# A gated recurrence's levels sent to TensorE in pairs, with a second pair of operand tiles

## The chip, the cores and the metric

The kernel runs on one core of one Trainium2 chip, in one launch. The metric is the device time of one execution in microseconds; the figure of a kernel is the median of several runs. A profiled execution gives the trace, whose own time and span (from the first to the last instruction) are given below. Engines are named as in the profile: PE is TensorE, PEld its weight loads, DVE is VectorE, ACT is ScalarE, POOL is GpSimd, SP is SyncE, which issues the transfers.

## The reference

One layer over 256 tokens of width 1024: an embedding layer norm, one input projection `w_in` into the columns of four causal mixers (Mamba-2 SSD, HGRN2, RetNet retention, MoBA attention), each with four heads of 64 and a gate, then one output projection, a residual and a layer norm. The part that the change touches, cut down:

```python
# HGRN2: S_t = diag(f_t) S_{t-1} + (1 - f_t) i_t^T, o_t = S_t^T q_t
att = einsum('bhtd,bhsd,bhtsd->bhts', q, k, exp(b_t - b_s))   # s <= t, b = cumsum(log f)
o   = einsum('bhts,bhsv->bhtv', att, v) + (carry of earlier chunks)

# SSD: causal depthwise convolution over 4 taps, then silu
xbc = silu(conv(xbc_raw, conv_w) + conv_b)

# MoBA, one block of 256 here: softmax over the causal scores with ALiBi
p = softmax(q k^T * d**-0.5 - slope * (t - s))
```

## The kernel before

**Slots.** The input projection is cut into 30 slots, two for each of 15 units of weights (`h_f`, `h_q`, `h_i`, `m_q`, `m_k`, `xs`, `bc`, `zv` twice, `r_q`, `r_k`, `r_v`, `m_g`, `gg` twice); eight more slots lie in the output projection. A slot is `begin(slot)` and then `project(slot)`. `begin` issues the load of the weights six slots ahead (`load_w`, SP), rounds the weights four slots ahead into a high part (`split_hi`, one cast on ACT, line 225), runs the list `steps[slot]`, and takes the low part on DVE (`split_lo`, line 234). `project` is 24 matmuls on PE (line 420; 12 a slot for the wide units `zv` and `gg`, line 381). The order of each engine's instructions is this program order, written out by hand in the table `steps`. Nothing overtakes on an engine: an instruction that waits holds all that is behind it there.

**The recurrence.** HGRN2's attention matrix is built by doubling. `A` (query side) and `B` (the tile `kk`, key side) hold operands decayed to block borders; `Fm[m]` holds the products of gates over blocks of m. `level(m)`, `level32`, `level64` and `level128` are the matmuls of B with A that give the entries between neighbouring blocks of m tokens; `widen(m)` multiplies half of A and half of B in place by the gates of the neighbouring block (three DVE operations, lines 524, 525 and 528), after which they stand for 2m. So the chain is widen, level, widen, level, and each widen has to wait until the level before it has read its operands. `level_in(m)` (DVE, line 552) writes the entries of a level into `att`; `level32_in` (ACT, lines 569 and 572) copies `att` and level 32 into `yh`; `level64_in` and `level128_in` (ACT, lines 587 and 600) copy the last two levels into `yh` and `l128`. `hgrn_av` in slot 20 reads `yh` and `l128`.

**The other steps near it.** `conv(n, name)` is one step on ACT (line 654, scale and bias from the PSUM bank of the projection), followed by three taps on DVE (line 656); four of these, then `conv_silu` on ACT (line 660). `moba_max(T)` is DVE (line 849), `moba_exp(T)` ACT (line 860), which waits for it, `moba_scale(T)` DVE (line 877). `ssd_step_a` is one small DVE operation (line 681) and two small exponentials on ACT (lines 682 and 683), the second of which waits for it. `moba_v` (line 833) copies the second half of the projection `zv` over the tile `kk`.

**PSUM.** All results of PE lie in one pool `pp` of 8 tiles, one bank each. A new tile takes the bank whose last reader comes first in program order, and its first matmul waits for that reader. `bank(...)` and `pp.tile(...)` are the allocations. Each level takes two banks (one for each parity of the head).

Of the kernel before, what the change touches and what calls it, by code (L numbers as in the profile page):

```python
# [17 lines left out]
P = 128  # L18
SEQ = 256
# [103 lines left out]
def hybrid_layer(  # L123
# [13 lines left out]
    nc = tc.nc  # L137
# [318 lines left out]
    f = sb([P, 2, SEQ], "f")  # L456
    kk = sb([P, 2, SEQ], "kk")
    A = sb([P, 2 * SEQ], "A")
    qk = sb([P, 2, SEQ], "qk", tag="s2a")
    B = flat(kk)  # L460
    Fm = {1: flat(f)}
    att = sb([P, 8, 64], "att", tag="att")
    hb = {}
# [17 lines left out]
    def hgrn_query():  # L481
        for n in range(2):
            nc.vector.tensor_mul(qk[:, n, :], hq[n], kk[:, n, :])
        for n in range(2):
            nc.vector.tensor_mul(A[:, n * SEQ:(n + 1) * SEQ], hq[n], f[:, n, :])
        nc.vector.tensor_mul(flat(e1)[:, 0::2], A[:, 1::2], B[:, 0::2])

# [28 lines left out]
    def hix(T, h):  # L516
        return (h % 2) * 4 + T * 2 + h // 2

    def widen(m):
        nb = 2 * SEQ // (2 * m)  # L520
        Fv = Fm[m].rearrange("p (b two) -> p b two", two=2)
        Av = A.rearrange("p (b two m) -> p b two m", two=2, m=m)
        Bv = B.rearrange("p (b two m) -> p b two m", two=2, m=m)
        nc.vector.tensor_mul(Av[:, :, 1, :], Av[:, :, 1, :], Fv[:, :, 0:1].to_broadcast([P, nb, m]))
        nc.vector.tensor_mul(Bv[:, :, 0, :], Bv[:, :, 0, :], Fv[:, :, 1:2].to_broadcast([P, nb, m]))
        if m < 64:
            Fn = sb([P, nb], f"F{2 * m}")
            nc.vector.tensor_mul(Fn, Fv[:, :, 0], Fv[:, :, 1])
            Fm[2 * m] = Fn

    def ab(t, h, lo_, n_):
        r = 64 * (h % 2)
        o = (h // 2) * SEQ + lo_
        return t[r:r + 64, o:o + n_]

    def level(m):
        bs = [bank(f"lv{m}{par}") for par in range(2)]
        for T in range(NT):
            for n in range(2):
                for c in range(2):  # L540
                    for par in range(2):
                        o = T * P + c * 64
                        q = (T * 2 + n) * 64
                        h = 2 * n + par
                        nc.tensor.matmul(bs[par][c * 64:c * 64 + 64, q:q + 64],  # L545
                                         ab(B, h, o, 64), ab(A, h, o, 64), start=True, stop=True)
        hb[m] = bs

    def level_in(m):
        i = (1, 2, 4, 8, 16).index(m)  # L550
        for par in range(2):
            nc.vector.copy_predicated(att[:, par * 4:par * 4 + 4, :],
                                      lev[:, i, :].unsqueeze(1).to_broadcast([P, 4, 64]),
                                      heads(hb[m][par][:, 0:256]))

    def level32():
        hb[32] = [heads(bank(f"lv32{par}")) for par in range(2)]
        for T in range(NT):
            for n in range(2):
                for c in range(2):  # L560
                    for par in range(2):
                        o = T * P + c * 64
                        h = 2 * n + par
                        nc.tensor.matmul(hb[32][par][c * 64:c * 64 + 32, T * 2 + n, 32:64],
                                         ab(B, h, o, 32), ab(A, h, o + 32, 32), start=True, stop=True)

    def level32_in():
        for c in range(2):
# [15 lines left out]

    def level64_in():
        for par in range(2):
            nc.scalar.copy(yh[0:64, par * 4:par * 4 + 4, 64:128], heads(hb[64][par][par * 64:par * 64 + 64, 0:256]))

    l128 = sb([P, 4, P], "l128")

    def level128():
        hb[128] = [bank(f"lv128{par}") for par in range(2)]
        for n in range(2):
            for par in range(2):
                nc.tensor.matmul(hb[128][par][:, n * P:(n + 1) * P], ab(B, 2 * n + par, 0, P),
                                 ab(A, 2 * n + par, P, P), start=True, stop=True)

    def level128_in():
        for par in range(2):
            nc.scalar.copy(l128[:, par * 2:par * 2 + 2, :],  # L600
                           hb[128][par][:, 0:256].rearrange("p (a t) -> p a t", t=P))

    hv = sb([P, NT, DB], "hv", tag="hv")
    ho = sb([P, 8, HD], "ho")
# [410 lines left out]
    def out_norm(T):  # L1015
# [12 lines left out]
        for n, c in enumerate(range(0, DM, st)):  # L1028
# [8 lines left out]
    steps = {  # L1037
        0: [lambda: hgrn_gate(0), lambda: hgrn_gate(1)],
        1: [hgrn_key],
        4: [hgrn_query, lambda: widen(1)],  # L1040
        6: [moba_load],
        7: [lambda: hgrn_diag(qk, 0), lambda: hgrn_diag(e1, 8), lambda: level(2), h_values,
            hgrn_diag_in],
        8: [lambda: level_in(2), lambda: widen(2), moba_q],
        9: [lambda: level(4), lambda: widen(4)],
        10: [lambda: level_in(4), lambda: level(8), moba_k],
        11: [lambda: level_in(8), lambda: widen(8)],
        12: [lambda: level(16), lambda: moba_scores(0), lambda: conv(0, "xs")],
        13: [lambda: moba_max(0, (0, 1, 2, 3)), lambda: moba_exp(0, (0, 1, 2, 3)), ssd_step_a,
             lambda: level_in(16), lambda: widen(16), lambda: conv(1, "xs")],  # L1050
        14: [level32, lambda: moba_scores(1), lambda: conv(2, "bc"), level32_in],
        15: [lambda: moba_max(1, (0, 1)), lambda: moba_max(1, (2, 3)), lambda: moba_exp(1, (0, 1, 2, 3)),
             lambda: widen(32), lambda: conv(3, "bc"), lambda: moba_scale(0)],
        16: [level64, lambda: widen(64), lambda: conv_silu("xs", 0), lambda: conv_silu("bc", 2),
             level64_in, lambda: moba_scale(1)],
        17: [lambda: load_rows(0), ssd_step_b],
        18: [level128, ssd_scores, lambda: moba_tr(0), lambda: moba_tr(1), moba_v, level128_in,
             lambda: z_in(0), lambda: z_in(1), ssd_scores_in, lambda: moba_tr_in(0), lambda: moba_tr_in(1)],
        20: [ssd_xt, ssd_seg, ssd_exp, lambda: moba_tr(2), lambda: hgrn_av(0), lambda: hgrn_av(1),
             lambda: moba_tr_in(2), ret_load],  # L1060
# [92 lines left out]
```

## Time and profile before

| | us |
|---|---|
| median of 3 runs (149.34 to 149.35) | 149.35 |
| profiled execution, its own time | 149.55 |
| its span | 147.8 |
| PE busy | 136.7 |
| DVE busy | 116.3 |
| ACT busy | 75.1 |

Busy time counts instructions, not waits. The profiled execution takes 1.75 us more than its span, and 0.2 us more than the median. The mean granted clock of TensorE is 0.982 of full speed.

### The profile page before, as it was taken

To read this page: it belongs to the slowest core of one execution; us is meant where nothing else is said; L and a number is where in the kernel's file an instruction comes from. 1 tells how busy PE (TensorE), PEld (TensorE's weight loads), DVE (VectorE), ACT (ScalarE), POOL (GpSimd) and SP (SyncE) were. 2 spreads that over 40 slices of the span, in tenths; PEclk is the share of its full clock that TensorE was granted. 3 is DMA by queue.
4 is the path that set the end of the run, shared out by engine and by line. 5 is a ranking of instruction groups with operands and counts; after the bars stand their busy time and mean duration, and the time that the engine had idled before them with its cause. 6 is when DMAs were issued, how large, how long until landed. Compare 5 with 4: busy or idle time off the path is not lost.

```text
span 147.8 us, 3075 instructions
## 1 busy us (share of the span) xinstructions
PE 136.7 (92%) x1224; PEld 122.4 (83%) x1224; DVE 116.3 (79%) x244; ACT 75.1 (51%) x122; POOL 16.0 (11%) x21
## 2 busy tenths in 40 slices
PE   5759999999999999999999999999999999999900
PEld 3159999999999998878899999999988888888900
DVE  1689978999597297969997599976989993959381
ACT  3079968662452759599808971035855655000000
POOL 4230000000000000000052009005002200002010
PEclk9977999999999999999999999999999999999997
DMA  4999299998758422494635740079874540000304
GB/s 146 287 381 361 63 302 356 299 344 316 217 153 248 143 48 94 142 244 190 162 119 146 265 163 4 0 231 357 278 233 156 162 155 0 0 0 0 142 0 142
DMA packets 9533, 26.05 MB, mean 176 GB/s; under 512 B 1072, under 2 KB 1968, under 8 KB 9264
## 3 DMA queue, kind: packets, MB, share of 16 engines
q1 hardware_dynamic: 9088, 25.35, 52.6%
q10 hardware_dynamic: 432, 0.52, 1.0%
q8 instruction: 9, 0.15, 0.4%
q14 instruction: 4, 0.03, 0.1%
HBM read 24.82 MB, written 1.05 MB: 175 GB/s over the span
## 4 chain that ended last, share of the span: by engine, by line
PE 82%; DVE 8%; DMA 3%; ACT 1%; SPq 1%; issue 1%; POOL 1%; DVEq 0%
PE po L996 15%; PE pj_gg L381 8%; PE pj_h_f L346 4%; PE pj_xs L420 4%; PE pj_m_k L420 4%; PE pj_m_g L420 4%; PE pj_r_k L420 4%; PE pj_m_q L420 4%; PE pj_h_i L420 4%; PE pj_zv L381 4%; PE pj_h_q L420 4%; PE pj_r_v L420 4%; PE pj_r_q L420 4%; DMA xt<-in_x_dram 3%; PE pj_bc L420 2%; PE lv L545 2%
## 5 line engine op out<-in xcount | busy, mean ns | idle before, releaser
L996 PE MATMUL po<-whi_wo,yhi 128*128 128x512 f32 (+1 forms) x40 | 14.0, 350 | 0.0
L996 PE MATMUL po<-wlo_wo,yhi 128*128 128x512 f32 (+1 forms) x40 | 14.0, 349 | 0.0
L996 PE MATMUL po<-whi_wo,ylo 128*128 128x512 f32 (+1 forms) x40 | 13.9, 348 | 0.0
L234 DVE TENSOR_TENSOR wlo_wo<-wr_wo,whi_wo 128x1024 fp32r<-128x1024 f32 x8 | 9.7, 1217 | 0.0
L225 ACT CAST whi_wo<-wr_wo 128x1024 fp32r<-128x1024 f32 x8 | 8.2, 1049 | 2.2 <-PE pj_gg L381 1.7
L996 PEld LDWEIGHTS po<-whi_wo,yhi 128*128 128x128 f32 x40 | 7.5, 188 | 1.1
L996 PEld LDWEIGHTS po<-wlo_wo,yhi 128*128 128x128 f32 x40 | 7.5, 188 | 1.0
L996 PEld LDWEIGHTS po<-whi_wo,ylo 128*128 128x128 f32 x40 | 7.5, 188 | 1.0
L710 POOL TENSOR_SCALAR_AFFINE_SELECT ra<-ahi 128x1024 fp32r<-128x1024 f32 x1 | 1.1, 1101 | 64.9 <-DVE ahi L706 64.9
L225 ACT CAST whi_zv<-wr_zv 128x1024 fp32r<-128x1024 f32 x4 | 4.2, 1048 | 6.8 <-PE pj_xs L420 3.4
L656 DVE SCALAR_TENSOR_TENSOR cacc_xs<-pj_xs,ch,cacc_xs 128x255 f32<-128x255 f32 (+2 forms) x6 | 2.9, 482 | 4.7 <-ACT cacc_xs L654 4.6
L381 PE MATMUL pj_zv<-whi_zv,hhi 128*128 128x512 f32 x16 | 6.5, 406 | 0.0
L179 PE MATMUL warm<-warm 128*128 128x512 f32 x6 | 5.1, 1011 | 1.5 <-DVE warm L176 1.5
L381 PE MATMUL pj_gg<-whi_gg,hhi 128*128 128x512 f32 x16 | 6.4, 398 | 0.0
L381 PE MATMUL pj_zv<-whi_zv,hlo 128*128 128x512 f32 x16 | 6.3, 394 | 0.0
L381 PE MATMUL pj_gg<-whi_gg,hlo 128*128 128x512 f32 x16 | 6.3, 394 | 0.0
L381 PE MATMUL pj_gg<-wlo_gg,hhi 128*128 128x512 f32 x16 | 6.3, 392 | 0.0
L381 PE MATMUL pj_zv<-wlo_zv,hhi 128*128 128x512 f32 x16 | 6.3, 392 | 0.0
L303 PE MATMUL tr<-ck,xn 128*128 128x128 f32 x16 | 3.7, 360 | 2.3 <-DVE xn L279 2.3
L303 PEld LDWEIGHTS tr<-ck,xn 128*128 128x128 f32 x16 | 2.6, 187 | 3.7 <-DVE xn L279 3.7
L225 ACT CAST whi_gg<-wr_gg 128x1024 fp32r<-128x1024 f32 x4 | 4.2, 1045 | 2.4 <-DMA wr_gg<-in_w_dram 1.6
L266 DVE BATCH_NORM_STATS2 lst<-xt 128x6 f32<-128x512 f32 x4 | 2.8, 694 | 3.2 <-DMA xt<-in_x_dram 3.2
(284 smaller groups left out, 490.4 us busy)
## 6 DMA issues: line engine op xcount, KB each, us to landing
wr_wo<-in_wo_dram SPq DMA_DIRECT2D x8, 512.0 KB, 3.9
wr_zv<-in_w_dram SPq DMA_DIRECT2D x4, 512.0 KB, 4.6
rb<-in_rows_dram SPq DMA_DIRECT2D x2, 1024.0 KB, 6.6
wr_gg<-in_w_dram SPq DMA_DIRECT2D x4, 512.0 KB, 4.9
wr_h_i<-in_w_dram SPq DMA_DIRECT2D x2, 520.0 KB, 5.2
xt<-in_x_dram SPq DMA_DIRECT2D x4, 256.0 KB, 3.5
wr_h_f<-in_w_dram SPq DMA_DIRECT2D x4, 256.0 KB, 4.7
wr_h_q<-in_w_dram SPq DMA_DIRECT2D x2, 512.0 KB, 5.5
```

The costliest lines, as they stand in the source:

```text
L179: nc.tensor.matmul(wb, warm[:, :P], warm, start=True, stop=True)
L225: copy(whi[i, j][:, r, :], t[:, r, :])
L234: nc.vector.tensor_sub(wlo[i, j][:, r, :], t[:, r, :], whi[i, j][:, r, :].bitcast(F32))
L266: nc.vector.bn_stats(lst[T][:, hf, :], xt[T][:, hf * 512:hf * 512 + 512])
L303: nc.tensor.transpose(trb[k][:, T * P:(T + 1) * P], xn[T][:, k * P:(k + 1) * P], ident)
L346: nc.tensor.matmul(ps[n], l[:, n * P:(n + 1) * P], r[:, k, :], start=(k == 0 and q == 0), stop=(k == KT - 1 and q == 2))
L381: nc.tensor.matmul(ps_of[name, T], l[:, k, ts], r, start=(k == 0 and q == 0), stop=(k == KT - 1 and q == 2))
L420: nc.tensor.matmul(ps, l, r, start=(n == 0), stop=(n == len(seq) - 1))
L545: nc.tensor.matmul(bs[par][c * 64:c * 64 + 64, q:q + 64], ab(B, h, o, 64), ab(A, h, o, 64), start=True, stop=True)
L656: nc.vector.scalar_tensor_tensor(a_[:, d:], ps[:, :SEQ - d], tap(3 - d), a_[:, d:], op0=ALU.mult, op1=ALU.add)
L710: nc.gpsimd.affine_select(out=t, in_=src.bitcast(F32).unsqueeze(2).to_broadcast([P, 8, P]), pattern=[[0, 8], [1, P]], compare_op=ALU.is_ge ...
L996: nc.tensor.matmul(po[T, c0], l[:, k, ts], r, start=(i == 0 and j == 0 and q == 0), stop=(last and q == 2), skip_group_check=(T == 1 and i ...
```

## The change

Three things in the source. First, the levels go to PE in pairs, 4 with 8, 16 with 32 and 64 with 128, each pair into one pair of banks (columns 0 to 255 and 256 to 511). Second, a second set of operands `AB[1]` (in the memory of the tile `ldec`, which is free until slot 20) takes every second widened pair: `widen(m, s, d)` reads set s and writes set d; where they differ, ACT copies the two halves that stay as they are. Third, the table of steps is rewritten: among other moves, `conv(1)` and `conv(3)` now stand before `moba_exp(0)` and `moba_exp(1)`, `ssd_step_a` after `conv(1)`, `level32_in` moves from slot 14 to 17, `level64` from 16 to 18.

```diff
-    def widen(m):
+    def widen(m, s, d):
         nb = 2 * SEQ // (2 * m)
+        if d == len(AB):
+            t = sb([P, 2, 2 * SEQ], "AB2", tag="ldec")
+            AB.append((t[:, 0, :], t[:, 1, :]))
...
+        if s != d:
+            nc.scalar.copy(Ad[:, :, 0, :], As[:, :, 0, :])
+            nc.scalar.copy(Bd[:, :, 1, :], Bs[:, :, 1, :])
+        nc.vector.tensor_mul(Ad[:, :, 1, :], As[:, :, 1, :], Fv[:, :, 0:1].to_broadcast([P, nb, m]))
+        nc.vector.tensor_mul(Bd[:, :, 0, :], Bs[:, :, 0, :], Fv[:, :, 1:2].to_broadcast([P, nb, m]))
...
+    def lv(m, after=None):
+        if after is None:
+            hb["b", m] = [bank(f"lv{m}{par}") for par in range(2)]
+        o = 0 if after is None else 256
+        hb[m] = [b[:, o:o + 256] for b in hb["b", m if after is None else after]]
+        return hb[m]
...
-        8: [lambda: level_in(2), lambda: widen(2), moba_q],
-        9: [lambda: level(4), lambda: widen(4)],
-        10: [lambda: level_in(4), lambda: level(8), moba_k],
-        11: [lambda: level_in(8), lambda: widen(8)],
-        12: [lambda: level(16), lambda: moba_scores(0), lambda: conv(0, "xs")],
-        13: [lambda: moba_max(0, (0, 1, 2, 3)), lambda: moba_exp(0, (0, 1, 2, 3)), ssd_step_a,
-             lambda: level_in(16), lambda: widen(16), lambda: conv(1, "xs")],
-        14: [level32, lambda: moba_scores(1), lambda: conv(2, "bc"), level32_in],
-        15: [lambda: moba_max(1, (0, 1)), lambda: moba_max(1, (2, 3)), lambda: moba_exp(1, (0, 1, 2, 3)),
-             lambda: widen(32), lambda: conv(3, "bc"), lambda: moba_scale(0)],
-        16: [level64, lambda: widen(64), lambda: conv_silu("xs", 0), lambda: conv_silu("bc", 2),
-             level64_in, lambda: moba_scale(1)],
-        17: [lambda: load_rows(0), ssd_step_b],
-        18: [level128, ssd_scores, lambda: moba_tr(0), lambda: moba_tr(1), moba_v, level128_in,
+        8: [lambda: widen(2, 0, 0), lambda: widen(4, 0, 1), lambda: level_in(2), moba_q],
+        10: [moba_k],
+        11: [lambda: level(4, 0), lambda: level(8, 1, 4), lambda: moba_scores(0),
+             lambda: level_in(4), lambda: level_in(8), lambda: widen(8, 1, 1)],
+        12: [lambda: conv(0, "xs"), lambda: widen(16, 1, 0), lambda: moba_max(0, (0, 1, 2, 3))],
+        13: [lambda: conv(1, "xs"), lambda: moba_exp(0, (0, 1, 2, 3)), ssd_step_a],
+        14: [lambda: level(16, 1), lambda: level32(0, 16), lambda: moba_scores(1),
+             lambda: conv(2, "bc"), lambda: widen(32, 0, 0), lambda: level_in(16)],
+        15: [lambda: widen(64, 0, 1), lambda: conv(3, "bc"), lambda: moba_max(1, (0, 1)),
+             lambda: moba_max(1, (2, 3)), lambda: moba_exp(1, (0, 1, 2, 3))],
+        16: [lambda: conv_silu("xs", 0), lambda: conv_silu("bc", 2), lambda: moba_scale(0),
+             lambda: moba_scale(1)],
+        17: [lambda: load_rows(0), level32_in, ssd_step_b],
+        18: [lambda: level64(0), lambda: level128(1), ssd_scores, lambda: moba_tr(0), lambda: moba_tr(1),
+             moba_v, level64_in, level128_in,
              lambda: z_in(0), lambda: z_in(1), ssd_scores_in, lambda: moba_tr_in(0), lambda: moba_tr_in(1)],
```

## Rows read from the trace of the kernel before

**Rows 1.** The page: part 1 (busy, share, instructions) and the chain by engine.

```profile
PE 136.7 (92%) x1224; PEld 122.4 (83%) x1224; DVE 116.3 (79%) x244; ACT 75.1 (51%) x122; POOL 16.0 (11%) x21
...
PE 82%; DVE 8%; DMA 3%; ACT 1%; SPq 1%; issue 1%; POOL 1%; DVEq 0%
```

**Rows 2.** The chain in order of time around level 4: start, us, what.

```profile
37.06 2.80 PE pj_m_k L420 x24
39.86 0.62 PE lv L545 x32
40.49 3.04 PE pj_m_k L420 x24
```

**Rows 3.** Timeline of PE, level 64 and slot 18: start, us, what, idle.

```profile
64.53 0.77 PE L582 MATMUL lv<-A,kk 64*64 64x64 f32 x16 [0.20 <-DVE F L528]
...
73.11 0.37 PE L420 MATMUL pj_r_q<-hhi,whi_r_q 128*128 128x256 f32 x1
```

**Rows 4.** Timeline of DVE, 50 to 64 us: start, us, what.

```profile
50.67 1.52 DVE L656 SCALAR_TENSOR_TENSOR cacc_xs<-pj_xs,ch,cacc_xs 128x255 f32<-128x255 f32 x3 [3.72 <-ACT cacc_xs L654]
52.10 1.22 DVE L234 TENSOR_TENSOR wlo_zv<-wr_zv,whi_zv 128x1024 fp32r<-128x1024 f32 x1
53.24 0.28 DVE L849 CUSTOM_DVE_ANT_0 pe<-ms,ali 128x128 f32<-128x128 f32 x1
...
54.35 0.77 DVE L552 COPY_PREDICATED att<-lev,lv 128x256 f32<-128x256 int32 x2
55.02 0.42 DVE L524 TENSOR_TENSOR A<-A,F 128x256 f32<-128x256 f32 x1
...
55.69 0.17 DVE L528 TENSOR_TENSOR F<-F 128x16 f32<-128x16 f32 x1
...
61.86 0.42 DVE L849 CUSTOM_DVE_ANT_0 pe<-ms,ali 128x256 f32<-128x256 f32 x1
...
62.74 0.42 DVE L849 CUSTOM_DVE_ANT_0 pe<-ms,ali 128x256 f32<-128x256 f32 x1
```

**Rows 5.** Timeline of ACT, 58 to 73 us: start, us, what.

```profile
58.00 1.25 ACT L569 COPY yh<-att 64x512 f32<-64x512 f32 x2
59.27 1.09 ACT L572 COPY yh<-lv 32x128 f32<-32x128 f32 x4
...
62.87 0.51 ACT L860 ACTIVATE pe<-pe,mmax 128x256 f32<-128x256 f32 x1 [1.43 <-DVE mmax L853]
...
64.96 0.56 ACT L654 ACTIVATE cacc_bc<-pj_bc,ch 128x256 f32<-128x256 f32 x1
65.42 1.04 ACT L225 CAST whi_r_k<-wr_r_k 128x1024 fp32r<-128x1024 f32 x1
66.48 1.28 ACT L660 ACT_TABLE_LOAD   x1
67.77 0.63 ACT L660 ACTIVATE xc<-cacc_xs 128x512 f32<-128x512 f32 x1
...
68.83 0.74 ACT L587 COPY yh<-lv 64x256 f32<-64x256 f32 x2
69.48 1.04 ACT L225 CAST whi_r_k<-wr_r_k 128x1024 fp32r<-128x1024 f32 x1
70.43 1.04 ACT L225 CAST whi_r_v<-wr_r_v 128x1024 fp32r<-128x1024 f32 x1
71.73 0.65 ACT L833 COPY mv<-pj_zv 128x256 f32<-128x256 f32 x2 [0.26 <-PE lv L595]
72.26 0.67 ACT L600 COPY l<-lv 128x256 f32<-128x256 f32 x2
```

**Rows 6.** Timeline of PE at the start: the two idle stretches before the transposes.

```profile
8.56 0.66 PE L303 MATMUL tr<-ck,xn 128*128 128x128 f32 x4 [2.01 <-DVE xn L279]
9.56 1.54 PE L303 MATMUL tr<-ck,xn 128*128 128x128 f32 x6 [0.34 <-DVE xn L279]
```

**Rows 7.** Busy time by stretch, 9 to 13 us; PEclk is the granted clock.

```profile
9.00:13.00 4.00, 3.66 (x19) 3.45 (x18) 3.71 (x10) 3.49 (x9) 0.37 (x1) 0.57 1.00 373
```

More of the change, by code (lines that the diff above doesn't have):

```diff
@@ L459, in hybrid_layer @@
     qk = sb([P, 2, SEQ], "qk", tag="s2a")
-    B = flat(kk)
+    AB = [(A, flat(kk))]
     Fm = {1: flat(f)}
@@ L485, in hgrn_query @@
             nc.vector.tensor_mul(A[:, n * SEQ:(n + 1) * SEQ], hq[n], f[:, n, :])
-        nc.vector.tensor_mul(flat(e1)[:, 0::2], A[:, 1::2], B[:, 0::2])
+        nc.vector.tensor_mul(flat(e1)[:, 0::2], A[:, 1::2], AB[0][1][:, 0::2])
     def hgrn_diag(t, o0):
@@ L517, in hix @@
         return (h % 2) * 4 + T * 2 + h // 2
-    def widen(m):
+    def widen(m, s, d):
         nb = 2 * SEQ // (2 * m)
+        if d == len(AB):
+            t = sb([P, 2, 2 * SEQ], "AB2", tag="ldec")
+            AB.append((t[:, 0, :], t[:, 1, :]))
         Fv = Fm[m].rearrange("p (b two) -> p b two", two=2)
[L522 to L525, printed above, removed]
+        (As, Bs), (Ad, Bd) = ([t.rearrange("p (b two m) -> p b two m", two=2, m=m) for t in AB[i]]
+                              for i in (s, d))
+        if s != d:
[3 more added lines that the diff above has]
+        nc.vector.tensor_mul(Bd[:, :, 0, :], Bs[:, :, 0, :], Fv[:, :, 1:2].to_broadcast([P, nb, m]))
         if m < 64:
@@ L534, in ab, with level @@
         return t[r:r + 64, o:o + n_]
-    def level(m):
-        bs = [bank(f"lv{m}{par}") for par in range(2)]
+    def lv(m, after=None):
[4 more added lines that the diff above has]
+        return hb[m]
+    def level(m, s, after=None):
+        A_, B_ = AB[s]
+        bs = lv(m, after)
         for T in range(NT):
@@ L545, in level @@
                         nc.tensor.matmul(bs[par][c * 64:c * 64 + 64, q:q + 64],
-                                         ab(B, h, o, 64), ab(A, h, o, 64), start=True, stop=True)
-        hb[m] = bs
+                                         ab(B_, h, o, 64), ab(A_, h, o, 64), start=True, stop=True)
     def level_in(m):
@@ L553, in level_in, with level32 @@
                                       lev[:, i, :].unsqueeze(1).to_broadcast([P, 4, 64]),
-                                      heads(hb[m][par][:, 0:256]))
-    def level32():
-        hb[32] = [heads(bank(f"lv32{par}")) for par in range(2)]
+                                      heads(hb[m][par]))
+    def level32(s, after):
+        A_, B_ = AB[s]
+        hb[32] = [heads(b) for b in lv(32, after)]
         for T in range(NT):
@@ L564, in level32 @@
                         nc.tensor.matmul(hb[32][par][c * 64:c * 64 + 32, T * 2 + n, 32:64],
-                                         ab(B, h, o, 32), ab(A, h, o + 32, 32), start=True, stop=True)
+                                         ab(B_, h, o, 32), ab(A_, h, o + 32, 32), start=True, stop=True)
     def level32_in():
@@ L573, in level32_in, with level64 @@
                                hb[32][par][c * 64:c * 64 + 32, 0:4, 32:64])
-    def level64():
-        hb[64] = [bank(f"lv64{par}") for par in range(2)]
+    def level64(s):
+        A_, B_ = AB[s]
+        bs = lv(64)
         for T in range(NT):
@@ L581, in level64, with level128 @@
                     h = 2 * n + par
-                    nc.tensor.matmul(hb[64][par][par * 64:par * 64 + 64, q:q + 64], ab(B, h, T * P, 64),
-                                     ab(A, h, T * P + 64, 64), start=True, stop=True)
+                    nc.tensor.matmul(bs[par][par * 64:par * 64 + 64, q:q + 64], ab(B_, h, T * P, 64),
+                                     ab(A_, h, T * P + 64, 64), start=True, stop=True)
     def level64_in():
         for par in range(2):
-            nc.scalar.copy(yh[0:64, par * 4:par * 4 + 4, 64:128], heads(hb[64][par][par * 64:par * 64 + 64, 0:256]))
+            nc.scalar.copy(yh[0:64, par * 4:par * 4 + 4, 64:128],
+                           heads(hb[64][par][par * 64:par * 64 + 64]))
     l128 = sb([P, 4, P], "l128")
-    def level128():
-        hb[128] = [bank(f"lv128{par}") for par in range(2)]
+    def level128(s):
+        A_, B_ = AB[s]
+        bs = lv(128, 64)
         for n in range(2):
             for par in range(2):
-                nc.tensor.matmul(hb[128][par][:, n * P:(n + 1) * P], ab(B, 2 * n + par, 0, P),
-                                 ab(A, 2 * n + par, P, P), start=True, stop=True)
+                nc.tensor.matmul(bs[par][:, n * P:(n + 1) * P], ab(B_, 2 * n + par, 0, P),
+                                 ab(A_, 2 * n + par, P, P), start=True, stop=True)
     def level128_in():
@@ L600, in level128_in @@
             nc.scalar.copy(l128[:, par * 2:par * 2 + 2, :],
-                           hb[128][par][:, 0:256].rearrange("p (a t) -> p a t", t=P))
+                           hb[128][par].rearrange("p (a t) -> p a t", t=P))
     hv = sb([P, NT, DB], "hv", tag="hv")
@@ L1039, in hybrid_layer @@
         1: [hgrn_key],
-        4: [hgrn_query, lambda: widen(1)],
+        4: [hgrn_query, lambda: widen(1, 0, 0)],
         6: [moba_load],
-        7: [lambda: hgrn_diag(qk, 0), lambda: hgrn_diag(e1, 8), lambda: level(2), h_values,
+        7: [lambda: hgrn_diag(qk, 0), lambda: hgrn_diag(e1, 8), lambda: level(2, 0), h_values,
             hgrn_diag_in],
-        8: [lambda: level_in(2), lambda: widen(2), moba_q],
-        9: [lambda: level(4), lambda: widen(4)],
-        10: [lambda: level_in(4), lambda: level(8), moba_k],
```

## The prediction

> **What bounds the kernel now.** I read the page first, then the chain, then the timelines of PE, DVE and ACT around the recurrence. PE is busy for 136.7 of 147.8 us, and the chain that ended last runs through it for 82% of the span [rows 1]. From the first transposes to the last matmul of the output projection PE works almost without a pause. The one wait in the part that changes is level 64's, 0.20 us for DVE's widening [rows 3]. So a microsecond taken from PE there is a microsecond of the kernel, and any wait that PE gets is paid in full, since nothing later has slack to give back. DVE and ACT set the time only where PE comes to wait for them. The question is therefore which result of DVE or ACT PE needs next, and by how much it is early.
>
> **What PE saves.** A projection's 24 matmuls take 2.80 us when no level stands in front of them and 3.04 us when one does [rows 2]; so one interruption by small matmuls costs 0.24 us beside its own 0.62 us. Before, the levels (with the small matmuls that go with them) interrupt in slots 9, 10, 12, 14, 16 and 18; after, in 11, 14 and 18. The matmuls stay the same in number and shape. Three interruptions less give 0.7 us, and level 64's wait of 0.20 us [rows 3] goes because `widen(32)` then has three slots of time. Together 0.9 us. The Trainium skill (TensorEngine Tiling (Array Packing), Key Properties) says that a change of tiling mode drains the engine, which would count changes of shape instead: 14 before and 10 after (a pair of 16 and 32 still has one inside). At half of 0.24 us for each the four would give 0.5 us instead of 0.7. I take the row's 0.7, as what is measured is the interruption as a whole.
>
> **What is added.** Six copies on ACT, two each in `widen(4)`, `widen(16)` and `widen(64)`. No row shows such a copy; the nearest is `moba_v`, two copies of the same 128x256 from PSUM in 0.53 us of the queue (71.73 to 72.26) [rows 5], so 0.27 us each. The upper bound is `conv`'s first step, of that size too, 0.46 us (64.96 to 65.42) [rows 5]. The pair costs 0.5 to 0.9 us of ACT. All three stand ahead of `moba_exp`, before which ACT waits for the maxima anyhow (1.43 us already before [rows 5]); that wait hides them, and without it each pair would cost its 0.5. DVE's widenings stay three operations each, written to another tile. Weight loads and their queue stay in order; `split_lo` of slot 11 comes later, but the weights whose buffer it frees are cast only after the exponentials, so nothing waits for them.
>
> **What moves: the work on DVE ahead of the second exponentials.** This is where I expect the loss. Before, nothing of levels 32 and 64 stands between `conv(0)`'s taps and `moba_max(1)`; after, `widen(32)`, `widen(64)` and, with them, `conv(3)` stand there. I add up DVE's queue from the first tap, in intervals from start to start. The taps wait for `xs` to be projected. Up to there PE has one interruption less (-0.24) and MoBA's first scores more (about a level's 0.62 [rows 2]), so they start 0.4 later than 50.67 [rows 4], at 51.05. Then, all from [rows 4]:
>
> - four convolutions at 1.43 (50.67 to 52.10): 5.72
> - three low parts of weights at 1.14 (52.10 to 53.24): 3.42
> - `moba_max(0)` and `ssd_step_a`'s small operation, 53.24 to 54.35: 1.11
> - `level_in(16)`, 54.35 to 55.02: 0.67
> - `widen(16)` and `widen(32)` at 0.67 (55.02 to 55.69) and 0.1 for F, `widen(64)` without F: 2.21
>
> That is 13.13 us without a wait. One wait comes in. `ssd_step_a`'s DVE operation now stands behind `conv(1)`'s taps, ending at about 57.0, and its exponential on ACT holds what is behind it there: a cast (0.95, 69.48 to 70.43) and `conv(2)`'s first step (0.56) [rows 5], so that step ends at about 58.7. DVE is ready for `conv(2)`'s taps at 58.1 and stands 0.6 to 0.7 us; I take 0.7. So `moba_max(1)` starts at 51.05 + 13.13 + 0.7 = 64.9, where it was 61.86 [rows 4]. The exponentials followed 1.01 us behind (62.87 [rows 5]); now they come at 65.9, three microseconds later, while PE is ahead of before.
>
> **The work on ACT behind them.** Between the exponentials and `l128`, ACT's queue is without a gap, as all that it needs is done by then. From [rows 5]: the four exponentials 2.09 (62.87 to 64.96), the cast of slot 16 with the silu's table behind it 1.06, the table 1.29, two silus 1.06 (67.77 to 68.83), the cast of slot 17 0.95, then `level32_in`, new at this place, 1.27 and 1.09, the cast of slot 18 0.95, `moba_v` 0.53, `level64_in` 0.65, and the first half of `level128_in` 0.37 (half of 0.67, and the latency). The sum is 11.3 us, so the first half of `l128` is there at 77.2. Before it was there at 72.6 (72.26 + 0.37).
>
> **Who waits for it.** In slot 18 the two banks of `zv`, two of levels 64 and 128, two of the SSD scores and two of MoBA's transposes fill all eight. So the projection `r_q` behind them can't start before one of these is read, and the first in the program to be given up is that of the first half of `l128`. The transposes themselves take the banks of levels 16 and 32, which `level32_in` now gives back in slot 17, at about 74.7 by the sum above; and the SSD scores wait for the silu at about 71.4. PE, which would be at `r_q` at 73.11 - 0.9 = 72.2 [rows 3], gets there at 77.3. It has the scores and transposes done in between, so it stands some 5 us in three pieces: the scores a little, the transposes over 2 us, `r_q` nearly 2 us. Before, the same bank was given back half a microsecond before `r_q` wanted it. From `r_q` on PE has its old work and no cover: the end moves by 77.3 - 73.1 = 4.2 us. In the profiled execution that is 149.55 + 4.2 = 153.75; the median lies 0.2 below it, so 153.55 us.
>
> **The clock on top.** PE stood 2.01 and then 0.34 us before the first transposes [rows 6], and after that its granted clock is 0.57 on average from 9 to 13 us [rows 7]: with levels of 1.2 and 2.4 GHz, the lower one for 0.86 of that time, 3.4 us, in which work worth 1.7 us is lost. The waits of slot 18 add up to more than that, around bursts of small matmuls like those transposes. I expect the clock to fall there too. The loss is 0 if the low stretch lies wholly in the waits, 1.7 if it lies wholly behind `r_q`'s start; nothing says which is nearer, so I take the middle, 0.85. The Trainium skill (TensorE: Matmul & The Clock Gate, HAM oscillation) tells of the same, matmul bursts with waits for data between them that start cold each time; by it too the loss belongs in the sum. No run here shows it in the middle of this kernel.
>
> The forecast: 149.35 + 4.2 + 0.85 = 154.4 us.
>
> **Rivals.**
>
> - *The clock holds.* PE waits as computed, at full clock: 153.55. For it: the clock falls nowhere else before the end, and three waits with work between them are shorter each than one of 5 us. Against: 2.01 and 0.34 us were enough at the start [rows 6, 7].
> - *ACT is in time, and the pairs pay.* The one mechanism is the bank that `r_q` takes. If `l128`'s first half is copied by 72.2, PE never waits and the kernel is faster by the 0.9 us: 148.45. That needs the exponentials 5 us sooner than 65.9, at 60.9, before they stood even in the old order (62.87 [rows 5]). For it: DVE stood 3.72 us before `conv(0)` [rows 4], so it is not always full. Against: that idle time lies ahead of the sum, not in it, and all 13 us of it are copied from rows.
> - *DVE's queue is shorter.* If `ssd_step_a` doesn't hold ACT, 0.7 less: 152.85 at full clock.
> - *The pairs don't save.* If level 8 had to wait at PE for ACT's copies and the taps, the 0.9 would be gone, but ACT and DVE set `r_q`'s start, so the forecast would stay at 154.4. Only if the waits of slot 18 were also about 0.9 would the time be as before; I see no row for that.
>
> **Chances and range.** A change under 0.2% can't be told from none here. The forecast with a falling clock 0.58, the clock holds 0.27, the shorter queue 0.07, in time and faster 0.06, no change 0.02. So faster 0.06, same 0.02, slower 0.92. From the shorter queue with some rounding (152.6) to the full loss of clock (153.55 + 1.7 = 155.25) with 0.9 for copies that cost more, or a second low stretch: 156.2.
>
> **What would show it.** In the new trace: `r_q`'s first matmul at 77 to 78 us, with an idle time before it that ends with ACT's `l128` copy; an idle time before the transposes `mpt` that ends with ACT's `yh` copies; the second exponentials at about 66; DVE full from 51 to 70 but for a short wait at `conv(2)`; levels 4 and 8 back to back at about 45.5; from `r_q` to the last matmul the same stretch as before, plus what the clock takes. Wrong would be: `r_q` at 72 to 73 and no wait of PE, or a wait that ends with another engine, or the exponentials near 62.

## The result, and the profile after

After the change the kernel takes 155.09 us (median of 4 runs), before it 149.35 us (4 runs beside them). The ratio is 1.0373, with a 95% interval from 1.0332 to 1.0414. The forecast was 154.4 us. The profiled execution of after took 154.22 us. Of the experiments below, one execution of e6_max_first and two of e8_in_time_conv_back took over 1.5% longer than the fastest of their kernel and are left out of the medians.

The page, its part 1 and the chain by engine; before is in [rows 1]:

```profile
PE 138.0 (91%) x1224; PEld 124.4 (82%) x1224; DVE 116.6 (76%) x244; ACT 77.2 (51%) x128; POOL 15.7 (10%) x21
...
PE 78%; DVE 9%; ACT 8%; DMA 2%; issue 1%; DVEq 0%; SPq 0%
```

PE has the same 1224 matmuls and ACT six copies more. The chain shows what changed: ACT's share of it has grown from 1% to 8%, and the span by 4.7 us. So PE now waits for ACT. Where it waits stands in the timeline of PE (start, us, what, idle time before it and what ended that); these rows answer to [rows 2, 3]:

```profile
68.19 0.68 PE L601 MATMUL lv<-A,kk 64*64 64x64 f32 x16
68.81 0.71 PE L616 MATMUL lv<-AB 64*128 64x128 f32 x8
70.23 0.94 PE L767 MATMUL scg<-xc 64*128 64x128 f32 x12 [0.71 <-ACT xc L681]
72.89 1.97 PE L887 MATMUL mpt<-ck,pe 128*128 128x128 f32 x8 [1.72 <-ACT yh L590]
76.20 0.58 PE L420 MATMUL pj_r_q<-hhi,whi_r_q 128*128 128x256 f32 x1 [1.35 <-ACT l L621]
```

Three waits in slot 18, each ended by ACT: the SSD scores for the silu, the transposes `mpt` for `yh`, `r_q` for `l128`. Level 64's wait has gone. The eight transposes take 1.97 us: in e1_copy_early below they take 1.09.

This execution starts its work earlier than the profiled one of before did, since the head of the kernel varies: the first matmul `pc` of slot 7 (the recurrence's first) starts at 31.51 here and at 32.35 there, and between 31.51 and 32.97 in all the traces. From the timeline of PE in after, then in before:

```profile
31.51 0.63 PE L502 MATMUL pc<-ck,qk 128*64 128x2 f32 x16
...
87.07 0.39 PE L420 MATMUL pj_r_k<-hhi,whi_r_k 128*128 128x256 f32 x1
```

```profile
32.35 0.63 PE L500 MATMUL pc<-ck,qk 128*64 128x2 f32 x16
...
71.49 0.84 PE L746 MATMUL scg<-xc 64*128 64x128 f32 x12
...
82.42 0.39 PE L420 MATMUL pj_r_k<-hhi,whi_r_k 128*128 128x256 f32 x1
```

So 0.84 us has to be added to a start of after to compare it with one of before: `r_q` at 77.04, where it was 73.11, a shift of 3.93 us. The saving on PE is there too: PE is ready for the SSD scores `scg` at 69.52 (70.23 less the wait of 0.71), 38.01 us behind `pc`, where before has 39.14. That is 1.13 us early, and PE then loses 5.06 us up to `r_q`.

The timeline of DVE, which answers to [rows 4]:

```profile
49.99 1.52 DVE L677 SCALAR_TENSOR_TENSOR cacc_xs<-pj_xs,ch,cacc_xs 128x255 f32<-128x255 f32 x3 [0.89 <-ACT cacc_xs L675]
...
57.62 1.52 DVE L677 SCALAR_TENSOR_TENSOR cacc_bc<-pj_bc,ch,cacc_bc 128x255 f32<-128x255 f32 x3 [0.54 <-ACT cacc_bc L675]
...
63.70 0.42 DVE L870 CUSTOM_DVE_ANT_0 pe<-ms,ali 128x256 f32<-128x256 f32 x1
```

From the first tap to `moba_max(1)` it is 13.71 us with one wait of 0.54 in it, at `conv(2)`. The timeline of ACT, which answers to [rows 5]:

```profile
55.98 0.21 ACT L704 ACTIVATE ex<-au 128x8 f32<-128x8 f32 x1 [0.81 <-DVE au L702]
...
59.56 0.41 ACT L531 COPY AB<-A 128x256 f32<-128x256 f32 x1 [1.03 <-DVE A L533]
59.92 0.41 ACT L532 COPY AB<-kk 128x256 f32<-128x256 f32 x1
60.23 0.56 ACT L675 ACTIVATE cacc_bc<-pj_bc,ch 128x256 f32<-128x256 f32 x1
64.70 0.51 ACT L881 ACTIVATE pe<-pe,mmax 128x256 f32<-128x256 f32 x1 [3.91 <-DVE mmax L874]
...
72.30 1.08 ACT L590 COPY yh<-lv 32x128 f32<-32x128 f32 x4
...
75.78 0.65 ACT L621 COPY l<-lv 128x256 f32<-128x256 f32 x2
```

ACT stands 3.91 us in front of the exponentials and has no gap behind them. Busy time by stretch, with the granted clock in the column behind POOL, which answers to [rows 7]:

```profile
69.00:72.00 3.00, 1.46 (x20) 1.08 (x18) 2.69 (x11) 2.96 (x6) 0.00 (x0) 1.00 0.63 182
72.00:73.00 1.00, 0.11 (x1) 0.11 (x2) 0.83 (x7) 0.93 (x4) 0.00 (x0) 0.87 0.90 360
73.00:79.00 6.00, 4.65 (x21) 4.25 (x22) 4.50 (x7) 5.92 (x16) 3.13 (x2) 0.50 0.30 90
79.00:80.00 1.00, 1.00 (x8) 1.00 (x8) 0.73 (x1) 0.23 (x1) 0.00 (x0) 0.71 0.00 0
```

The clock falls to its lower level (0.50, 1.2 GHz) during the second wait and comes back within 79 to 80. The starts on PE give what that costs. From the first matmul of `r_q` to the first of `r_k` after takes 10.87 us (76.20 to 87.07) and before 9.31 (73.11 to 82.42), with the same instructions in between: the clock costs 1.56 us here. From `r_k` to the first matmul of `gg` both take 23.84 us.

### The profile page after: what moved, and what is told of

Its sections match the earlier page's. It is cut to its first block, busy times and chain, and to the rows that moved or that the text cites. A ratio compares the mean times of both kernels' runs of the same rounds, so it can differ in the third digit from the quotient of the medians.

```text
span 152.5 us, 3079 instructions
## 1 busy us (share of the span) xinstructions
PE 138.0 (91%) x1224; PEld 124.4 (82%) x1224; DVE 116.6 (76%) x244; ACT 77.2 (51%) x128; POOL 15.7 (10%) x21
## 3 DMA queue, kind: packets, MB, share of 16 engines
HBM read 24.82 MB, written 1.05 MB: 170 GB/s over the span
## 4 chain that ended last, share of the span: by engine, by line
PE 78%; DVE 9%; ACT 8%; DMA 2%; issue 1%; DVEq 0%; SPq 0%
PE po L1017 15%; PE pj_gg L381 7%; PE pj_r_q L420 5%; PE pj_h_f L346 4%; PE pj_m_g L420 4%; PE pj_r_k L420 4%; PE pj_xs L420 4%; PE pj_m_q L420 4%; PE pj_h_i L420 4%; PE pj_h_q L420 4%; PE pj_r_v L420 4%; PE pj_m_k L420 4%; PE pj_bc L420 4%; DMA xt<-in_x_dram 2%; PE tr L303 2%; DVE cacc_bc L677 2%
## 5 line engine op out<-in xcount | busy, mean ns | idle before, releaser
L420 PE MATMUL pj_r_q<-hhi,whi_r_q 128*128 128x256 f32 x16 | 5.3, 333 | 1.3 <-ACT l L621 1.3
L234 DVE TENSOR_TENSOR wlo_zv<-wr_zv,whi_zv 128x1024 fp32r<-128x1024 f32 x4 | 4.9, 1221 | 1.5 <-ACT whi_zv L225 1.5
L179 PE MATMUL warm<-warm 128*128 128x512 f32 x6 | 4.3, 876 | 1.5 <-DVE warm L176 1.5
L881 ACT ACTIVATE pe<-pe,mmax 128x128 f32<-128x128 f32 (+1 forms) x8 | 3.5, 445 | 3.9 <-DVE mmax L874 3.9
```

Source lines behind the costliest of these rows:

```text
L179: nc.tensor.matmul(wb, warm[:, :P], warm, start=True, stop=True)
L234: nc.vector.tensor_sub(wlo[i, j][:, r, :], t[:, r, :], whi[i, j][:, r, :].bitcast(F32))
L420: nc.tensor.matmul(ps, l, r, start=(n == 0), stop=(n == len(seq) - 1))
```

## The experiments

Theory: ACT's late `level32_in` and `level128_in`, late because of the exponentials, because of DVE's queue, hold PE in slot 18, and the clock falls on top. Rivals: the banks alone, the clock alone, the convolutions' place, or pairs that save nothing.

The table compares by a measure without the head: from the start of `pc` (slot 7) to that of `r_k` (slot 22), and from there to `gg`. "Clock" is the time from `r_q` to `r_k` above its 9.31 us (above 10.34 where the transposes `mpt` have been moved into that stretch); the ratios are against the kernel before, measured beside each.

| kernel | median (runs) | ratio [95%] | `pc` to `r_k`, against before | `r_k` to `gg` | clock |
|---|---|---|---|---|---|
| before | | | 50.07 | 23.84 | 0.0 |
| after | 155.09 (4) | 1.0373 [1.0332, 1.0414] | +5.49 | 23.84 | 1.56 |
| e1_copy_early | 150.98 | 1.0097 [1.0075, 1.0119] | +1.52 | 23.84 | 0.0 |
| e2_banks | 152.21 | 1.0176 [1.0134, 1.0217] | +2.93 | 23.83 | 1.27 |
| e3_keep_busy | 154.05 | 1.0302 [1.0278, 1.0325] | +4.60 | 23.84 | 0.0 |
| e4_in_time | 148.98 (10) | 0.9975 [0.9947, 1.0002] | -1.13 | 23.87 | 0.0 |
| e5_before_copy_late | 151.18 | 1.0115 [1.005, 1.018] | +1.63 | 23.84 | 0.0 |
| e6_max_first | 151.33 (3) | 1.012 [1.0053, 1.0187] | +1.88 | 23.83 | 0.0 |
| e7_conv_back | 155.75 | 1.0406 [1.0325, 1.0488] | +5.06 | 23.84 | 1.50 |
| e8_in_time_conv_back | 150.6 (2) | 1.008, no interval | +1.19 | 23.89 | 0.0 |
| e9_in_time_again | 149.45 (12) | 0.9998 [0.9975, 1.0021] | -1.09 | 24.86 | 0.0 |
| e10_in_time_table | 148.29 (6) | 0.9915 [0.9884, 0.9946] | -1.09 | 23.88 | 0.0 |
| e11_before_table | 149.46 (12) | 0.9992 [0.9971, 1.0013] | +0.03 | 23.84 | 0.0 |

Where no number of runs is given it is 4. The clock shows 0.0 where the difference is under 0.1; in e8_in_time_conv_back that stretch is 1.85 us longer, but with waits in it and the clock at 1.00.

**One copy moved back (e1_copy_early).** After, with `level32_in` alone put ahead of the second exponentials.

```diff
-        15: [..., lambda: moba_max(1, (2, 3)), lambda: moba_exp(1, (0, 1, 2, 3))],
+        15: [..., lambda: moba_max(1, (2, 3)), level32_in, lambda: moba_exp(1, (0, 1, 2, 3))],
-        17: [lambda: load_rows(0), level32_in, ssd_step_b],
+        17: [lambda: load_rows(0), ssd_step_b],
```

> The changed kernel with one step moved: level32_in stands in slot 15 ahead of moba_exp(1), where ACT stood 3.91 us waiting for the maxima, and no longer in slot 17. Theory 'late on ACT': the six copies take 2.4 us out of the queue between the second exponentials and l128, the wait of the transposes (1.72 us) is gone, r_q starts about 2.4 us earlier (at 73.8 where it was 76.2) after a wait of about 1.9 us; with the clock held 151.0 us, with a low stretch up to 152.7. Rival 'the pairs and the second set cost': the place of six copies changes nothing, 155.1 us.

Measured 150.98 us. The timeline of its PE:

```profile
71.18 0.94 PE L767 MATMUL scg<-xc 64*128 64x128 f32 x12 [0.70 <-ACT xc L681]
72.05 1.09 PE L887 MATMUL mpt<-ck,pe 128*128 128x128 f32 x8
74.76 0.38 PE L420 MATMUL pj_r_q<-hhi,whi_r_q 128*128 128x256 f32 x1 [1.62 <-ACT l L621]
```

The wait at the transposes has gone, that at `r_q` stays, and the clock holds. One line of the table of steps carries about 4 of the 5.5 us: 2.4 of shift and 1.56 of clock.

**The banks (e2_banks).** After, with the first eight transposes and their copies moved to the head of slot 20, so that slot 18 needs six banks and `r_q` doesn't wait for `l128`.

```diff
-        18: [..., ssd_scores, lambda: moba_tr(0), lambda: moba_tr(1), moba_v, ..., ssd_scores_in,
-             lambda: moba_tr_in(0), lambda: moba_tr_in(1)],
-        20: [ssd_xt, ssd_seg, ...
+        18: [..., ssd_scores, moba_v, ..., ssd_scores_in],
+        20: [lambda: moba_tr(0), lambda: moba_tr(1), lambda: moba_tr_in(0), lambda: moba_tr_in(1),
+             ssd_xt, ssd_seg, ...
```

> The changed kernel with MoBA's transposes of slot 18 and their copies moved to the head of slot 20, so that r_q takes a bank of levels 16 and 32, given back by level32_in, and not one of levels 64 and 128. Theory 'r_q waits for its bank alone': r_q starts at about 73.0, right behind the first copies of level 32, and not at 76.2 behind l128, though l128 comes no earlier; the transposes' 0.9 us then lie in slot 20. About 2.3 us off the 155.1, 152.8 us, and less if the clock holds (151.0). Rival 'r_q waits for the data of ACT's queue as a whole': r_q stays at 76, and the time at 155.1 or over.

```profile
70.68 0.94 PE L767 MATMUL scg<-xc 64*128 64x128 f32 x12 [0.72 <-ACT xc L681]
73.34 0.58 PE L420 MATMUL pj_r_q<-hhi,whi_r_q 128*128 128x256 f32 x1 [1.72 <-ACT yh L590]
```

Measured 152.21 us, and `r_q` came 41.39 us behind `pc`, where after has 44.69. `r_q` now waits for `yh`, whose bank it took over, as long as the transposes did. The waiter is whoever asks for the next bank; the cause is the late copy. The clock fell here too, with two waits in place of three.

**The clock alone (e3_keep_busy).** After, with 20 matmuls that compute nothing behind the scores and 24 behind the transposes, in the scores' banks.

```diff
+    def keep_busy(g, n):
+        for _ in range(n):
+            nc.tensor.matmul(sd["sc"][g][:, 3, :], hhi[:, 0, 0:P], hhi[:, 1, 0:P], start=True, stop=True)
...
-        18: [..., ssd_scores, lambda: moba_tr(0), lambda: moba_tr(1),
+        18: [..., ssd_scores, lambda: keep_busy(0, 20), lambda: moba_tr(0), lambda: moba_tr(1),
+             lambda: keep_busy(1, 24),
```

> The changed kernel with 20 matmuls of 128 columns, whose results nobody reads, behind the SSD scores and 24 more behind the transposes, in PE's waits of slot 18. They add work and change no order of ACT or DVE. Theory 'the clock fell because PE stood': the granted clock stays at 1.00 in the waits and behind them, r_q still starts at about 76, its 48 matmuls take 5.6 us instead of 7.4, and the kernel is 1.8 us faster than the changed one, 153.3 us. Rival 'the low stretch costs little, and the rest of the loss is elsewhere': the clock stays up and the time is within 0.5 us of 155.1.

```profile
71.83 2.45 PE L1060 MATMUL scg<-hhi 128*128 128x128 f32 x20
74.11 1.06 PE L887 MATMUL mpt<-ck,pe 128*128 128x128 f32 x8
74.93 2.87 PE L1060 MATMUL scg<-hhi 128*128 128x128 f32 x24
```

Measured 154.05 us, a gain of 0.9 by the head-free measure where 1.8 was expected. The clock stayed at 1.00 through slot 18 and `r_q`, which returns the 1.56 us; but the 20 took 2.28 us (71.83 to 74.11) and the 24 2.71, and so pushed `r_q` 0.7 us past its bank (45.39 us behind `pc`, where after has 44.69). So the clock's share is real, and the dummies were sized too long.

**The exponentials earlier (e6_max_first).** After, with `moba_max(1)` first in slot 15, ahead of `widen(64)` and `conv(3)`.

```diff
-        15: [lambda: widen(64, 0, 1), lambda: conv(3, "bc"), lambda: moba_max(1, (0, 1)),
-             lambda: moba_max(1, (2, 3)), lambda: moba_exp(1, (0, 1, 2, 3))],
+        15: [lambda: moba_max(1, (0, 1)), lambda: moba_max(1, (2, 3)),
+             lambda: widen(64, 0, 1), lambda: conv(3, "bc"), lambda: moba_exp(1, (0, 1, 2, 3))],
```

> The changed kernel with moba_max(1) first in slot 15, ahead of widen(64) and conv(3) on DVE; ACT's order stays. Theory 'late on ACT, because DVE has 13 us ahead of the maxima': the exponentials start 2.1 us earlier, and so do the transposes and r_q (74.1 where it was 76.2), behind a wait of 0.7 and one of 2.2 us: 153.0 us, and 151.3 if the clock holds. Rival 'the exponentials' start is not what the queue waits for': under 0.5 us.

```profile
71.65 1.20 PE L887 MATMUL mpt<-ck,pe 128*128 128x128 f32 x8 [0.60 <-ACT yh L590]
74.96 0.39 PE L420 MATMUL pj_r_q<-hhi,whi_r_q 128*128 128x256 f32 x1 [2.11 <-ACT l L621]
```

`r_q` came 42.59 us behind `pc`, 2.1 us sooner than in after, and the clock held. DVE's queue ahead of the maxima is the source of that part.

**The late copy without the pairs (e5_before_copy_late).** The kernel before, with `level32_in` alone moved from slot 14 to 17.

```diff
-        14: [level32, lambda: moba_scores(1), lambda: conv(2, "bc"), level32_in],
+        14: [level32, lambda: moba_scores(1), lambda: conv(2, "bc")],
-        17: [lambda: load_rows(0), ssd_step_b],
+        17: [lambda: load_rows(0), level32_in, ssd_step_b],
```

> The kernel before, without pairs, second set or earlier convolutions, with one step of the change alone: level32_in moves from slot 14 to slot 17. Theory 'late on ACT': the six copies now stand between the exponentials and l128 there too; r_q, which had half a microsecond to spare, starts about 1.6 us later, and as the wait is short the clock holds: 1.6 us over the kernel before. Rival 'it takes the pairs to lose': no change beside the kernel before.

```profile
74.99 0.38 PE L420 MATMUL pj_r_q<-hhi,whi_r_q 128*128 128x256 f32 x1 [1.36 <-ACT l L600]
```

Measured 1.8 us slower (151.18 against 149.4), 1.63 on the trace. The old kernel has the same wall half a microsecond away, and needs no pairs to run into it.

**The convolutions back (e7_conv_back).** After, with `conv(1)` and `conv(3)` behind the exponentials again and `ssd_step_a` ahead of `conv(1)`.

```diff
-        13: [lambda: conv(1, "xs"), lambda: moba_exp(0, (0, 1, 2, 3)), ssd_step_a],
+        13: [lambda: moba_exp(0, (0, 1, 2, 3)), ssd_step_a, lambda: conv(1, "xs")],
-        15: [lambda: widen(64, 0, 1), lambda: conv(3, "bc"), ..., lambda: moba_exp(1, (0, 1, 2, 3))],
+        15: [lambda: widen(64, 0, 1), ..., lambda: moba_exp(1, (0, 1, 2, 3)), lambda: conv(3, "bc")],
```

> The changed kernel with conv(1) and conv(3) put back behind moba_exp(0) and moba_exp(1), and ssd_step_a ahead of conv(1), the third part of the change undone alone. Theory 'late on ACT': widen(64) stays ahead of the maxima, DVE now waits about 1.3 us for conv(1)'s first step, so the exponentials start only 0.8 us earlier, and conv(3)'s first step then stands in ACT's queue behind them for 0.5 us; r_q starts 0.4 us earlier and the time is 154.7 us. Rival 'the convolutions ahead of the exponentials are the loss': most of the 5.7 us come back, under 151 us.

Measured 155.75 us; `r_q` came 44.32 us behind `pc`, where after has 44.69, and PE waits at the same three places (0.35, 1.72 and 1.34 us). The convolutions' place is worth 0.4 us at `r_q`, and is not the loss. The trace bears out the 0.4 us that were expected; the median, above after's 155.09, doesn't show them (its four runs reach from 154.33 to 156.4).

**Everything in time (e4_in_time, then e9_in_time_again).** After, with the maxima first in slot 15, `level32_in` behind `conv(3)` there, `level64_in` and `level128_in` ahead of `moba_v`, and the eight transposes in slot 20.

```diff
+        15: [lambda: moba_max(1, (0, 1)), lambda: moba_max(1, (2, 3)), lambda: widen(64, 0, 1),
+             lambda: conv(3, "bc"), level32_in, lambda: moba_exp(1, (0, 1, 2, 3))],
...
+        18: [lambda: level64(0), lambda: level128(1), ssd_scores,
+             level64_in, level128_in, moba_v, lambda: z_in(0), lambda: z_in(1), ssd_scores_in],
...
```

> The changed kernel with pairs, second set and convolutions as they are, but with ACT in time: moba_max(1) first in slot 15, level32_in there too, level64_in and level128_in ahead of moba_v, and the transposes at the head of slot 20. Theory 'late on ACT': PE has no wait over 0.2 us from slot 8 to slot 22, the clock stays up, and the 0.9 us of the pairs show: 148.5 us. Rival 'the pairs and the second set cost': still slower than before, over 150 us.

PE doesn't wait between slots 7 and 22, and reaches `r_k` 1.13 us earlier than before: the pairs pay once the copies are in time. On this trace the gain still stands at `gg` (1.10 us), but DVE's `rat`, which PE's `reo` reads (RetNet's masked scores and its output matmuls), ends only at 103.97, when `reo` has begun with the first half of it:

```profile
102.69 1.28 DVE L961 TENSOR_TENSOR rat<-rs,ck 128x512 f32<-128x512 f32 x2
...
103.86 1.67 PE L452 MATMUL reo<-rv,rat 128*64 128x64 f32 x48
```

The median of its ten runs (148.98 us, ratio 0.9975) doesn't show a full microsecond. The same kernel with more runs:

> The kernel of e4_in_time once more, for a narrower interval. Between the recurrence's first matmuls of slot 7 and the first of r_k its profile took 48.94 us where the kernel before took 50.07. If that is what the pairs are worth, the time lies 0.4 to 1.1 us below the kernel before on the same chip, a ratio of 0.993 to 0.997. If the gain is given back later, the ratio is 1.

The time was 149.45 us, that of before (ratio 0.9998). The table of measures says where the gain went: the trace reaches `r_k` 1.09 us early and then takes 24.86 in place of 23.84 us to `gg`. The timelines of DVE and PE in that stretch:

```profile
84.95 0.69 DVE L934 TENSOR_TENSOR rq<-pj_r_q,ret 128x512 f32<-128x512 f32 x1 [4.18 <-DMA ret<-in_ret_dram]
...
103.50 1.28 DVE L961 TENSOR_TENSOR rat<-rs,ck 128x512 f32<-128x512 f32 x2
...
104.33 0.34 PE L452 MATMUL reo<-rv,rat 128*64 128x64 f32 x4 [0.36 <-ACT whi_gg L225]
104.84 1.50 PE L452 MATMUL reo<-rv,rat 128*64 128x64 f32 x44 [0.17 <-DVE rat L961]
```

The table `ret` lies in memory that the transposes `mpt` read until slot 20, so its load is issued only then (79.77 us here, 80.97 before) and took 5.09 us (4.1 in e4_in_time, 3.6 before). `rq`, RetNet's scaled queries, waits for it; all that DVE has to do behind `rq` is late; and `rat` ends at 104.78, past the time PE wants it. The first 0.36 us of PE's wait the profile puts down to ACT's cast of weights for `gg`, which ends at 104.28, the first half of `rat` at 104.18; these two aren't told apart, and both come 3.0 us earlier behind `pc` in e10_in_time_table below. The same rows of the kernel before, from its timelines of DVE and PE:

```profile
84.67 0.69 DVE L913 TENSOR_TENSOR rq<-pj_r_q,ret 128x512 f32<-128x512 f32 x1 [1.65 <-DMA ret<-in_ret_dram]
...
103.21 1.28 DVE L940 TENSOR_TENSOR rat<-rs,ck 128x512 f32<-128x512 f32 x2
...
104.71 1.62 PE L452 MATMUL reo<-rv,rat 128*64 128x64 f32 x48
```

There `rat` ends at 104.49 and PE starts `reo` at 104.71: 0.2 us of slack.

**The second wall taken away (e10_in_time_table and e11_before_table).** The same kernel with `ret` in memory of its own and its load at the end of slot 18; and the kernel before with that alone.

```diff
-    ret = sb([P, 2, 2, SEQ], "ret", tag="xt0")
+    ret = sb([P, 2, 2, SEQ], "ret")
-        18: [..., lambda: z_in(0), lambda: z_in(1), ssd_scores_in],
+        18: [..., lambda: z_in(0), lambda: z_in(1), ssd_scores_in, ret_load],
-             lambda: moba_tr_in(2), ret_load],
+             lambda: moba_tr_in(2)],
```

> Compared with e4_in_time only the table `ret` moves: it gets memory of its own, and its load is issued at the end of slot 18 (about 71 us) in place of slot 20 (79.8). Theory (the table's transfer is the second wall: the pairs, put in time, gain about 1.1 us up to the recurrence's end, but DVE's chain rq, ret, rat behind the transfer is only 0.3 us ahead of PE at reo): rq no longer waits for a DMA, PE waits nowhere at reo, and the gain shows: about 148.4 us, ratio about 0.993. Rival (the gain is lost elsewhere, or was only a difference between executions): ratio 0.998 to 1.000 again, with or without a wait at reo.

> Kernel before, with the same move of `ret` alone. Theory: PE reached reo 0.3 us after DVE had finished rat, so nothing waits there and an earlier table frees nothing on PE's path: 149.2 to 149.5 us, ratio 0.998 to 1.001. Rival (the table's transfer costs time in the kernel before as well, so a gain of e10_in_time_table would be the table's and not the pairs'): 148.8 or less, ratio below 0.996.

```profile
80.32 0.68 DVE L934 TENSOR_TENSOR rq<-pj_r_q,ret 128x512 f32<-128x512 f32 x1
...
100.12 1.28 DVE L961 TENSOR_TENSOR rat<-rs,ck 128x512 f32<-128x512 f32 x2
...
103.37 1.62 PE L452 MATMUL reo<-rv,rat 128*64 128x64 f32 x48
```

These are rows of e10_in_time_table: `rq` no longer waits for the transfer, `rat` ends 2 us ahead of `reo`, and the time is 148.29 us, ratio 0.9915 [0.9884, 0.9946]. The move by itself does nothing in the kernel before (0.9992 [0.9971, 1.0013]). So the pairs, with the order that puts ACT in time, gain 1.05 us up to `gg` on the trace (1.35 between the medians), and they need both walls out of the way. This version is faster than both kernels.

**A miss (e8_in_time_conv_back).** The in-time kernel of e4_in_time with the convolutions behind the exponentials again.

> The kernel of e4_in_time with conv(1) and conv(3) behind the exponentials, and ssd_step_a ahead of conv(1). It tells what that part of the change is worth when ACT is in time. By the queues' sums DVE has 1.6 us less to spare at conv(3) and the SSD scores wait 0.3 us for the silu: 0.3 us over e4_in_time. If the convolutions' place decides, over 1 us more than e4_in_time.

```profile
79.06 0.96 PE L752 MATMUL seg<-ra,upr 128*128 128x512 f32 x3 [0.87 <-POOL ra L731]
81.44 0.80 PE L452 MATMUL hgo<-hv,yh 128*64 128x64 f32 x20 [0.82 <-ACT mpt L891]
```

On the trace it is 2.3 us slower than e4_in_time up to `r_k`, where 0.3 was expected; the ratio on record, 1.0174 [1.0087, 1.026], is higher than the 1.008 of the two executions in the table (150.18 and 151.01 us). My sum stopped at slot 18. The waits are in slot 20, where PE now wants POOL's `ra` and ACT's `mpt`. The traces agree with a delay that goes from the convolutions' late taps through DVE to these: `conv(3)`'s taps start 34.79 us behind `pc` (32.49 in e4_in_time), `ra` 44.14 (41.82) and the copy of `mpt` 49.08 (46.75), 2.3 us later each. No run isolates it.

## Why the prediction was right, step by step

- **The wall.** Right: `r_q` ends its wait on ACT's `l128` copy, at 77.04 in the time of before (76.20 + 0.84), where the forecast had 77.3. A shift of 3.93 us, forecast 4.2.
- **DVE's queue.** Right: 13.71 us from the first tap to `moba_max(1)`, forecast 13.13 + 0.7; the wait at `conv(2)` is 0.54. ACT's 0.81 us in front of `ssd_step_a`'s exponential put the cast and `conv(2)`'s first step behind it at 57.03; MoBA's scores on PE end at 57.02 by the chain, so that `ssd_step_a` alone is the cause isn't shown. The exponentials stand at 65.54 in the time of before (forecast 65.9).
- **ACT's queue.** Right: 11.46 us from the exponentials to the end of `l128`'s first half (64.70 to 76.16 by the chain), forecast 11.3.
- **The copies.** Those of `widen(64)` cost 0.67 us of the queue (59.56 to 60.23), inside the bounds of 0.5 and 0.9, and ACT's idle 3.91 us hides them.
- **The waits.** In place, but shorter in all: 0.71, 1.72 and 1.35 make 3.78 us, forecast some 5. PE's whole loss there is 5.06 us: the transposes at the lower clock (1.97 in place of 1.09 us) fill part of what was counted as waiting, and `r_q`'s start is not moved by that, since ACT sets it.
- **The clock.** The mechanism was right, the term mis-sized: taken as 0.85 us, the middle of 0 to 1.7, it measured 1.56, near the upper bound. That the bound held is luck: it was half of a low stretch of 3.4 us, as at the start, and here the lower level lasted 6.8 us, from inside the second wait (72.75) to 79.58; but the transposes and the third wait took half of it, and 3.4 us lay over `r_q`. The 1.56 us are one execution's: the four of after have mean clocks of 0.951, 0.966, 0.967 and 0.953 at 154.22, 155.1, 155.91 and 155.08 us, so the higher clocks didn't come with the shorter times, and what the other three lost here isn't known. That e3_keep_busy gets `r_q` to `r_k` back to 9.28 us shows the cost apart from the waits. The rule of the Trainium skill that the forecast named (TensorE: Matmul & The Clock Gate, HAM oscillation), bursts with waits between them that start cold, has longer waits in its own case than any here; it is borne out by after, e2_banks and e7_conv_back, but not by e1_copy_early and e6_max_first, whose bursts with waits of 0.70 and 1.62, or 0.60 and 2.11 us, stayed at 1.00.
- **The sum.** On the trace 3.93 + 1.56 = 5.49 us, forecast 4.2 + 0.85 = 5.05; between the medians 5.74. The shift came out 0.27 less and the clock 0.71 more than forecast, so two misses cancel in part. The 0.25 us left is within what the executions differ by (after's four reach from 154.22 to 155.91).
- **The pairs.** Forecast to save 0.9 us on PE, measured 1.09 to 1.13 up to `r_k` in the three in-time profiles, and 1.13 up to the SSD scores in after itself. The order of other steps was changed in all of them and no run has the pairs alone, so this is an upper reading of the pairs.
- **A step that failed.** "A microsecond taken from PE there is a microsecond of the kernel" is false for a gain. The rival in which the pairs pay was priced at 148.45 us; the kernel that fulfils its condition takes 148.98 and 149.45, because DVE's chain behind `ret` stood only 0.2 us ahead of PE: in one trace the gain still reached `gg`, in the other it was given back. That step played no part in the forecast itself, where PE came later and the chain had room.

## What to carry to other kernels

A step moved later on a helper engine costs what its result's next reader has to wait, and with all PSUM banks taken the reader is whatever asks for the next bank, not the step named in the code: sum the helper's queue to that bank. Before counting a gain on the bounding engine, look for the next engine's distance behind it: here 0.2 us ahead of `reo`, so that a saved microsecond wasn't safe until a transfer elsewhere was issued earlier. When short waits with small matmuls between them appear, add the slower clock over the next full stretch as a term of its own, with a chance: it fell in three of the six kernels that the next section lists.

## What the runs showed of the hardware that was not expected

The granted clock fell in three kernels whose waits in slot 18 were 0.71, 1.72 and 1.35 us (after), 0.72 and 1.72 (e2_banks), 0.35, 1.72 and 1.34 (e7_conv_back), and held at 1.00 with 0.70 and 1.62 (e1_copy_early), 0.60 and 2.11 (e6_max_first) and 1.36 alone (e5_before_copy_late). Neither the longest wait nor the sum sorts them: e6_max_first has 2.71 us in all and held, e2_banks 2.44 and fell. In the three that fell nothing but the scores (0.94 us) stood between the first two waits listed there, in e1_copy_early and e6_max_first the transposes as well or alone. Whether that is the cause was not tried, and it may not be all of it: the four executions of e2_banks have mean clocks of 0.961 to 0.980, with 152.81 us at 0.962 and 151.31 at 0.980. That is a hint that one kernel loses the clock in some executions and not in others, not a reading, since the mean also counts the end of an execution, where PE has no work left.

Matmuls of half the columns were not cheaper: the 20 dummies of 128 columns started 0.114 us apart (2.28 us for 20), the 128x256 matmuls of `r_q` at full clock 0.118 (5.68 us for 48 in e1_copy_early, 74.76 to 80.44).
